# Group B's attention in a one-core decoder layer: stacked float32r scores, and two heads' value products in turns

## The chip, the cores and the metric

The kernel runs on one core of a Trainium2 chip. The metric is the time of one execution on the device, in microseconds; where several runs of a kernel are shown, their median. The engines are TensorE (PE, with its weight loads PEld), VectorE (DVE), ScalarE (ACT), GpSimd (POOL) and SyncE (SP), whose queue issues the transfers here.

## The reference, cut to what matters

One decoder layer on 512 tokens of width 1024, in float32. After an RMS norm one projection gives the inputs of two groups of 8 heads of width 64. Group A attends to the 128 keys per query that an indexer picks (top-k). Group B uses three dilated causal windows whose outputs are merged by their softmax denominators. Both outputs go through one output projection. Cross-attention into 256 memory tokens, a squared-ReLU MLP of width 4096 and a last norm follow.

```python
h = rmsnorm(x, norm_mix_g[l])
proj = h @ w_in[l]
o_a = dsa_sparse_attention(q_nope, q_rope, c_kv, k_rope, q_idx, k_idx, p_wi, w_uk[l], w_uv[l])
q_b = rope(qkv[:, :, 0]).transpose(0, 2, 1, 3)
k_b = rope(qkv[:, :, 1]).transpose(0, 2, 1, 3)
o_b = dilated_attention(q_b, k_b, v_b).transpose(0, 2, 1, 3)
x = x + heads @ w_out[l]
```

## The kernel before, in words

Tokens are taken in 4 tiles (t) or query blocks (b) of 128. Dense products are made of float32r parts: each operand is split into hi and lo, and `mm3` (L155) adds hi x hi, hi x lo and lo x hi, 8 chunks of the contraction each, into one PSUM bank of 512 columns. Weights come in units through three raw buffers on SP's queue (`load_weight`, L132); ScalarE or VectorE rounds hi, GpSimd or VectorE subtracts for lo (`split_unit`, L123). All matmuls are issued from one helper, L107, all transposes from L112, so the profile's rows are told apart by tiles: mm is a dense product, sc a score, tp a transpose, pv a value product.

PSUM has 3 banks for mm, 2 for tp, 2 for sc and 1 for pv.

Before the attention, lines 285 to 361 make the latents, the indexer's key and queries and its scores per block (`acc`). The indexer's queries are already stored as hi in partitions 0 to 63 and lo in 64 to 127 (L334 to L338). Then group B's values are projected (L364), and its queries and keys (L370 to L385): 8 heads at a time, a token tile each; `rope` (L256) rotates on VectorE into `tok`, four transposes follow, and ScalarE copies them (L383) into float32 tiles qB (buffer u2a) and kB (u2b), a pair of heads in the two halves of the partitions.

`attend` (L390) does one query block of one group, n = 128 (b + 1) keys. Head by head (two at a time in short blocks) it computes the scores, adds the bias and takes the row maximum on VectorE (L407), exponentials with their sums on ScalarE (L409), the reciprocal (L410) and the scaling (L412) on VectorE, transposes the probabilities in blocks of 128, and copies them from PSUM (pT): on ScalarE (L422) for group B, on VectorE (L420) for two thirds of group A's. The value products follow, one head's key blocks in a row, an even head in columns 0 to 63 of the array and an odd one in 64 to 127:

```python
for h, c in hs:
    r0 = (h % 2) * DH
    for kc in range(b + 1):
        mmul(pvv[r0:r0 + DH, h // 2, :], vtile[kc // 2][:, kc % 2, h * DH:(h + 1) * DH],
             pT[:, c.start + kc * P:c.start + (kc + 1) * P], start=kc == 0, stop=kc == b)
```

Group B's scores are float32 products on 64 rows of the array (`scores_b`, L436). Group A's have 96 rows (`scores_a`, L530).

Other parts: `queries_a` (L443) projects group A's queries, four heads at a time. `norm_mem` (L460) loads and normalises the memory tokens, the first of its two tiles in buffer ghi1. `keys_a` (L484) makes group A's keys and values from the latents. `top_k` (L521) runs 16 times a search for the 8 largest values and a replacement, on VectorE (L525, L526). `keys_cross` (L536) projects the memory's keys into u2a and u2b. The written order is group_b(0), queries_a(0), top_k(1), group_b(1), top_k(2), queries_a(1), memory, group_b(2), keys_a, top_k(3), group_b(3), then group A's blocks 0 to 3, keys_cross, and the output projection (`project_add`, L579), which needs both groups' heads of a token tile. This is not the order on the engines: the program is built with `schedule_with_timeline_sim=True`, and a planner that puts its own durations on instructions orders each engine's queue up to line 665; from there on products and transposes of some stages are kept in the written order (`ordered`). A queue works in order.

Of the kernel before, what the change touches and what calls it, by code (L numbers as in the profile page):

```python
# [11 lines left out]
F32 = mybir.dt.float32  # L12
# [5 lines left out]
P = 128  # L18
# [26 lines left out]
def shape_constants():  # L45
    """Tables that depend on positions alone: group B's log-multiplicity bias, the causal
    bias of a diagonal block, and the rotary cosines and sines."""
# [17 lines left out]
def kernel(  # L65
# [40 lines left out]
    def mmul(*a, **k):  # L106
        ins = nc.tensor.matmul(*a, **k)  # L107
        if ordered[0]:
            tc.keep_in_program_order(ins)

# [12 lines left out]
    def split_unit(raw, hi, lo, how="v"):  # L123
        """float32r hi and lo of raw; how names the engines: p the lo on GpSimd, v on VectorE,
        their capitals the hi on VectorE instead of ScalarE."""
        if how in "PV":
            nc.vector.tensor_copy(hi, raw)  # L127
        else:
            nc.scalar.copy(hi, raw)  # L129
        (nc.gpsimd if how in "pP" else nc.vector).tensor_tensor(lo, raw, f32(hi), op=ALU.subtract)  # L130

    def load_weight(w, segs, k0, how, between=None):  # L132
        """w [rows, cols] in DRAM; the column segments side by side, K chunks k0..k0+7.
        Returns (hi, lo): lists over the K chunks of [128, ncols] views."""
# [20 lines left out]
    def mm3(dst, a, b, first=True, last=True, ks=None):  # L155
        """dst += sum_k a_k^T b_k, a and b as (hi list, lo list); lo x lo is below float32."""
# [6 lines left out]
    # ---- RMS norms: the gain is applied where the rows are transposed; a row's 1/rms is kept  # L163
    # apart and applied where the row's products come back ----
# [19 lines left out]
    def mean_square(src, junk, n=D, scale=None):  # L184
        """Mean of a row's squares over n columns, as this part of it adds to it."""
        ms = small("ss")
        nc.scalar.activation(junk, src, AF.Square, scale=n ** -0.5 if scale is None else scale, accum_out=ms)
        return ms
# [13 lines left out]
    def transpose_half(rows, g0, his, los, bank=bank_tp):  # L202
        """rows [128 tokens, 4 chunks of 128] -> transposed, times the gain, as hi + lo per chunk."""
# [11 lines left out]
    # =============================== token mixing ===============================  # L215
# [4 lines left out]
    xa = [mtile([P, 2, D], F32, f"u2{c}") for c in "ab"]  # L220
    nc.sync.dma_start(xa[0][:, 0, 0:512], x_rows[:, 0, 0:512])
    load_gains([norm_mix_g], G_MIX)
    nc.sync.dma_start(xa[0][:, 0, 512:], x_rows[:, 0, 512:])
    w_in0 = w_in[0]

    def x_load(t):
        nc.sync.dma_start(xa[t // 2][:, t % 2, :], x_rows[:, t, :])
# [12 lines left out]
    for t in range(NT):  # L240
        xt = xa[t // 2][:, t % 2, :]
# [13 lines left out]

    def rope(ps, heads, half, tabs, t, dst, dup=None):  # L256
        """ps [128, heads, 2, half] (token rows, before the norm's 1/rms) -> dst like it, rotated
        by the token's position."""
# [3 lines left out]
        rb = tmp.tile([P, 512], F32, name=nm("rb"), tag="rb", bufs=2)  # L262
# [107 lines left out]
    qkB = []  # L370
    for tag, col in (("u2a", C_QB), ("u2b", C_KB)):
        dst = mtile([P, 4, S], F32, tag)
        wt = load_weight(w_in0, [(col, col + 512)], 0, "pppp")
        for t in range(NT):
# [8 lines left out]
            nc.scalar.copy(dst[:, :, t * P:(t + 1) * P], tp)  # L383
        qkB.append(dst)
    qB, kB = qkB  # L385
# [4 lines left out]
    def attend(b, scores, bias_of, scale, vtile, chunk0, pv):  # L390
        """One block of 128 queries, all heads of a group; leaves the heads' outputs transposed
        (features on partitions) in chunks chunk0.. of the output projection's input."""
        n = P * (b + 1)
        pvv = pv.rearrange("p (j t) -> p j t", j=4)
        per = 2 if b == 0 or b == 1 and chunk0 else 1
        order = list(range(NH)) if chunk0 == 0 else [
            q + r + 2 * i for q in range(0, NH, 2 * per) for r in range(2) for i in range(per)]
        for g in range(NH // per):
            hs = [(h, slice(n * i, n * i + n)) for i, h in enumerate(order[per * g:per * g + per])]
            ps = bank_s()  # L400
            for h, c in hs:
                scores(ps[:, c], b, h, n)
            pr = (att.tile([P, 512], F32, name=nm("p"), tag="ct0", bufs=1) if chunk0 == 0 and g % 4 == 3 else
                  att.tile([P, 512], F32, name=nm("p"), tag="p", bufs=3))
            mx, sm, rc = (small(k, 4)[:, :per] for k in ("mx", "sm", "rc"))
            for i, (h, c) in enumerate(hs):
                nc.vector.tensor_tensor_reduce(pr[:, c], ps[:, c], bias_of(b, n), op0=ALU.add, op1=ALU.min,  # L407
                                               scale=-scale, scalar=3.0e38, accum_out=mx[:, i:i + 1])
                nc.scalar.activation(pr[:, c], pr[:, c], AF.Exp, bias=mx[:, i:i + 1], scale=-1.0, accum_out=sm[:, i:i + 1])  # L409
            nc.vector.reciprocal(rc, sm)  # L410
            for i, (h, c) in enumerate(hs):
                nc.vector.tensor_scalar(pr[:, c], pr[:, c], rc[:, i:i + 1], None, op0=ALU.mult)  # L412
            tp = bank_tp()
            m = n * per
            for c in range(0, m, P):
                tpose(tp[:, c:c + P], pr[:, c:c + P], ident)
            pT = (att.tile([P, 512], F32, name=nm("pT"), tag="ct1", bufs=1) if chunk0 == 0 and g % 3 == 2 else
                  att.tile([P, 512], F32, name=nm("pT"), tag="pT", bufs=2))
            if chunk0 == 0 and g % 3 != 1:
                nc.vector.tensor_copy(pT[:, :m], tp[:, :m])  # L420
            else:
                nc.scalar.copy(pT[:, :m], tp[:, :m])  # L422
            for h, c in hs:
                r0 = (h % 2) * DH
                for kc in range(b + 1):
                    mmul(pvv[r0:r0 + DH, h // 2, :], vtile[kc // 2][:, kc % 2, h * DH:(h + 1) * DH],
                         pT[:, c.start + kc * P:c.start + (kc + 1) * P], start=kc == 0, stop=kc == b)
        for i in range(2):
            q = chunk0 // 2 + i
# [6 lines left out]
    def scores_b(dst, b, h, n):  # L436
        r0 = (h % 2) * DH
        mmul(dst, qB[r0:r0 + DH, h // 2, b * P:(b + 1) * P], kB[r0:r0 + DH, h // 2, :n],
                         start=True, stop=True)

# [33 lines left out]
    def group_b(b):  # L474
        attend(b, scores_b, lambda b, n: m3[:, 512 - n:], SC_B, vB, 4, bank("pv", 1))
# [8 lines left out]
    def keys_a():  # L484
        """Group A's keys and values from the latents."""
# [35 lines left out]
    def top_k(b):  # L521
# [5 lines left out]
        sel[b] = att.tile([P, n], F32, name=f"sel{b}")  # L527
# [315 lines left out]
```

## Time and profile before

| what | value |
|---|---|
| median of 3 runs | 846.05 us (845.87 to 847.75) |
| span of the profiled execution, first to last instruction | 843.6 us |
| the profiled execution's own time | not given apart from the span |
| PE busy | 821.7 us, 97% |
| DVE busy | 474.4 us, 56% |
| ACT busy | 331.4 us, 39% |
| POOL busy | 293.2 us, 35% |

A busy PE is not a PE at its peak: matmuls are pipelined and their ends are modelled, so the distance between the starts of records tells what one costs. The chain of waits follows the work that ended last back in time; where an engine's share stands on it, that engine's own work set the pace. A float32 product appears as two records, a float32r product as one.

### The profile page before, as it was taken

What the parts mean: (1) busy time and instruction counts of PE and PEld (TensorE: products, weight loads), DVE (VectorE), ACT (ScalarE), POOL (GpSimd) and SP (SyncE); (2) the same over time, 40 slices, a digit from 0 to 9 for tenths busy, and PEclk for the clock granted to TensorE, in tenths of its full rate; (3) what the DMA queues carried; (4) which work ended last, traced back from release to release, by engine and by line L of the source; (5) the groups of instructions that cost most, each with busy time, mean ns of one, the idle gap of its engine ahead of it and who ended that gap; (6) DMA issues with size and microseconds to landing.
All of it is one profiled execution on the core that took longest, in us unless ns stands there. A gap on an engine that the chain in (4) does not pass through costs nothing.

```text
span 843.6 us, 11086 instructions
## 1 busy us (share of the span) xinstructions
PE 821.7 (97%) x4182; PEld 679.2 (81%) x4182; DVE 474.4 (56%) x1010; ACT 331.4 (39%) x676; POOL 293.2 (35%) x179
## 2 busy tenths in 40 slices
PE   7899999999999999999999999999999999999997
PEld 6788787886787788788898878888888888888886
DVE  7876999998777634535673344423542244225413
ACT  5354424457754524223464433213431243123322
POOL 5734303131513405544501233333333333333351
PEclk9899999999999999999999999999999999999999
DMA  7443122112412303332510223333233322322202
GB/s 278 125 125 88 33 74 70 63 21 80 150 53 99 96 5 100 99 100 86 184 56 19 82 100 101 101 99 100 100 100 99 100 100 97 103 91 85 99 1 100
DMA packets 44516, 77.34 MB, mean 92 GB/s; under 512 B 4752, under 2 KB 10544, under 8 KB 44464
## 3 DMA queue, kind: packets, MB, share of 16 engines
q1 hardware_dynamic: 44464, 76.64, 27.8%
q8 instruction: 33, 0.54, 0.3%
q14 instruction: 19, 0.16, 0.1%
HBM read 74.01 MB, written 2.10 MB: 90 GB/s over the span
## 4 chain that ended last, share of the span: by engine, by line
PE 85%; DVE 11%; issue 1%; POOL 1%; ACT 1%; DMA 0%; SPq 0%; POOLq 0%; ACTq 0%; DVEq 0%
PE mm L107 71%; PE tp L112 5%; PE sc L107 5%; PE pv L107 4%; DVE m L525 1%; DVE ghi L360 1%; DVE tok L279 1%; DVE glo L526 1%; DVE rb L271 1%; DVE tok L271 1%; DVE whi L127 1%; DVE wlo L130 1%; DVE ghi L526 1%; DMA u2a<-in_x_dram 0%; DVE ghi L358 0%
## 5 line engine op out<-in xcount | busy, mean ns | idle before, releaser
L130 POOL TENSOR_TENSOR wlo<-wraw,whi 128x1024 fp32r<-128x1024 f32 (+2 forms) x107 | 256.2, 2408 | 404.5 <-ACT whi L129 318.8
L107 PE MATMUL mm<-whi,h 128*128 128x512 f32 (+2 forms) x624 | 200.1, 381 | 3.9 <-DVE h L213 2.0
L129 ACT CAST whi<-wraw 128x1024 fp32r<-128x1024 f32 (+3 forms) x111 | 114.3, 1030 | 149.6 <-PE mm L107 105.4
L107 PE MATMUL mm<-h,whi 128*128 128x512 f32 (+1 forms) x448 | 154.9, 369 | 0.0
L107 PE MATMUL mm<-wlo,h 128*128 128x512 f32 (+2 forms) x376 | 141.9, 379 | 0.2 <-DVE wlo L130 0.2
L107 PEld LDWEIGHTS mm<-whi,h 128*128 128x128 f32 x624 | 117.9, 195 | 22.0 <-ACT whi L129 2.2
L107 PE MATMUL mm<-u,whi 128*128 128x512 f32 x320 | 124.7, 390 | 0.0
L107 PE MATMUL mm<-u,wlo 128*128 128x512 f32 x320 | 123.5, 389 | 0.0
L107 PE MATMUL mm<-whi,ghi 128*128 128x512 f32 (+1 forms) x264 | 102.0, 390 | 0.0
L107 PE MATMUL mm<-whi,glo 128*128 128x512 f32 (+1 forms) x264 | 101.5, 385 | 0.0
L107 PE MATMUL mm<-wlo,ghi 128*128 128x512 f32 (+1 forms) x264 | 100.7, 383 | 0.0
L107 PEld LDWEIGHTS mm<-h,whi 128*128 128x128 f32 x448 | 81.1, 188 | 14.3 <-issue 1.0
L130 DVE TENSOR_TENSOR wlo<-wraw,whi 128x1024 fp32r<-128x1024 f32 (+2 forms) x24 | 62.2, 2591 | 37.5 <-ACT whi L129 37.5
L107 PEld LDWEIGHTS mm<-wlo,h 128*128 128x128 f32 x376 | 72.6, 194 | 11.1 <-DVE wlo L130 0.6
L107 PEld LDWEIGHTS mm<-u,whi 128*128 128x128 f32 x320 | 60.1, 188 | 12.4
L107 PEld LDWEIGHTS mm<-u,wlo 128*128 128x128 f32 x320 | 60.0, 188 | 12.5
L802 DVE TENSOR_TENSOR sq<-r 128x512 f32<-128x512 f32 x32 | 22.0, 689 | 66.7 <-ACT r L800 66.7
L107 PEld LDWEIGHTS mm<-whi,glo 128*128 128x128 f32 x264 | 49.6, 188 | 10.1 <-issue 0.2
L107 PEld LDWEIGHTS mm<-wlo,ghi 128*128 128x128 f32 x264 | 49.7, 188 | 9.6 <-issue 0.4
L107 PEld LDWEIGHTS mm<-whi,ghi 128*128 128x128 f32 x264 | 49.6, 188 | 9.4 <-issue 0.2
L409 ACT ACTIVATE p<-p,mx 128x128 f32<-128x128 f32 (+3 forms) x64 | 35.8, 560 | 29.4 <-DVE mx L407 28.5
L800 ACT ACTIVATE r<-mm 128x512 f32<-128x512 f32 x32 | 19.1, 598 | 64.8 <-PE mm L107 64.8
(212 smaller groups left out, 1116.7 us busy)
## 6 DMA issues: line engine op xcount, KB each, us to landing
wraw<-in_w_up_dram SPq DMA_DIRECT2D x32, 512.0 KB, 3.8
wraw<-in_w_down_dram SPq DMA_DIRECT2D x32, 512.0 KB, 3.6
wraw<-in_w_in_dram SPq DMA_DIRECT2D x16, 512.0 KB, 3.6
wraw<-in_w_kv_cross_dram SPq DMA_DIRECT2D x16, 512.0 KB, 3.9
wraw<-in_w_out_dram SPq DMA_DIRECT2D x8, 512.0 KB, 3.6
wraw<-in_w_q_cross_dram SPq DMA_DIRECT2D x8, 512.0 KB, 3.6
wraw<-in_w_o_cross_dram SPq DMA_DIRECT2D x8, 512.0 KB, 4.1
wraw<-in_w_in_dram SPq DMA_DIRECT2D x8, 256.0 KB, 2.9
```

Source lines behind the costliest of these rows:

```text
L107: ins = nc.tensor.matmul(*a, **k)
L112: ins = nc.tensor.transpose(*a, **k)
L127: nc.vector.tensor_copy(hi, raw)
L129: nc.scalar.copy(hi, raw)
L130: (nc.gpsimd if how in "pP" else nc.vector).tensor_tensor(lo, raw, f32(hi), op=ALU.subtract)
L271: nc.vector.scalar_tensor_tensor(o, i, r, tab, op0=ALU.mult, op1=ALU.mult)
L279: nc.vector.tensor_tensor(dst[:, :, c, :], ra[:, :, c, :], rbv[:, :, c, :], op=ALU.add)
L360: nc.vector.scalar_tensor_tensor(acc[b], rl[:, :n], wh, acc[b], op0=ALU.mult, op1=ALU.add)
L409: nc.scalar.activation(pr[:, c], pr[:, c], AF.Exp, bias=mx[:, i:i + 1], scale=-1.0, accum_out=sm[:, i:i + 1])
L526: nc.vector.match_replace(acc[b], m8, acc[b], GONE)
L800: nc.scalar.activation(r, ps, AF.Relu)
L802: nc.vector.tensor_tensor(sq, r, r, op=ALU.mult)
```

## The change

Group B's queries and keys are projected by four heads at a time (`heads_b(g)`, g = 0 and 1): a weight of 256 query and 256 key columns, kept transposed in one float32r tile, hi in partitions 0 to 63 and lo in 64 to 127, ScalarE writing hi and VectorE lo. For each query block two transfers on SP's queue write the queries with the halves exchanged (`qs`). A head's scores are two float32r products on all 128 rows: queries with keys (hi x hi and lo x lo), then exchanged queries with keys (lo x hi and hi x lo).

`attend` takes pairs of heads. In blocks 0 and 1 a pair shares one score bank, one probability tile and one copy, on ScalarE and VectorE in turns; in blocks 2 and 3 each head has its own, the first's copy on VectorE and the second's on ScalarE. The value products of the two heads are issued in turns, key block by key block, and the first one of a pair waits for both copies. There are 3 probability buffers in all (before 3, and one more for group A) and 4 of pT (before 2, and one more for group A).

The order of the work is new, as the diff's end shows. To make room, u2 becomes one buffer of 16 KB a partition, used by x, group B's first four heads, the second four, and keys_cross in that order; the rotation's scratch moves into buffer ghi1; the selection mask is bfloat16; two tiles of the residual are loaded into a pool that opens behind the attention's. Comments are removed.

```diff
...
-    xa = [mtile([P, 2, D], F32, f"u2{c}") for c in "ab"]
+    xa = mtile([P, NT, D], F32, "u2")
...
+    rbs = mtile([P, 2, 512], F32, "ghi1")
+    turn = [0]
     def rope(ps, heads, half, tabs, t, dst, dup=None):
         cos, sin, nsin = (tab[:, t, None, :].to_broadcast([P, heads, half]) for tab in tabs)
         r = r_mix[:, t:t + 1]
         n = heads * 2 * half
-        rb = tmp.tile([P, 512], F32, name=nm("rb"), tag="rb", bufs=2)
+        turn[0] ^= 1
+        rb = rbs[:, turn[0], :]
...
-    qkB = []
-    for tag, col in (("u2a", C_QB), ("u2b", C_KB)):
-        dst = mtile([P, 4, S], F32, tag)
-        wt = load_weight(w_in0, [(col, col + 512)], 0, "pppp")
+    def heads_b(g):
+        qk = mtile([P, NH, S], F32R, "u2")
+        wt = load_weight(w_in0, [(C_QB + 256 * g, C_QB + 256 * g + 256), (C_KB + 256 * g, C_KB + 256 * g + 256)], 0, "pppp")
         for t in range(NT):
             ps = bank_mm()
             mm3(ps, h_tok(t), wt)
...
             for j in range(4):
                 tpose(tp[:, j, :], tok[:, j * P:(j + 1) * P], ident)
-            nc.scalar.copy(dst[:, :, t * P:(t + 1) * P], tp)
-        qkB.append(dst)
-    qB, kB = qkB
+            for i in range(2):
+                src = tp[i * DH:(i + 1) * DH]
+                dst = qk[:, i::2, t * P:(t + 1) * P]
+                nc.scalar.copy(dst[0:DH], src)
+                nc.vector.tensor_tensor(dst[DH:P], src, f32(dst[0:DH]), op=ALU.subtract)
+        return qk
     heads_hi = [None] * 4
     heads_lo = [None] * 4
-    def attend(b, scores, bias_of, scale, vtile, chunk0, pv):
+    def attend(b, pairs, scores, bias_of, scale, vtile, q0):
         n = P * (b + 1)
-        pvv = pv.rearrange("p (j t) -> p j t", j=4)
-        per = 2 if b == 0 or b == 1 and chunk0 else 1
-        order = list(range(NH)) if chunk0 == 0 else [
-            q + r + 2 * i for q in range(0, NH, 2 * per) for r in range(2) for i in range(per)]
-        for g in range(NH // per):
-            hs = [(h, slice(n * i, n * i + n)) for i, h in enumerate(order[per * g:per * g + per])]
-            ps = bank_s()
-            for h, c in hs:
-                scores(ps[:, c], b, h, n)
-            pr = (att.tile([P, 512], F32, name=nm("p"), tag="ct0", bufs=1) if chunk0 == 0 and g % 4 == 3 else
-                  att.tile([P, 512], F32, name=nm("p"), tag="p", bufs=3))
-            mx, sm, rc = (small(k, 4)[:, :per] for k in ("mx", "sm", "rc"))
-            for i, (h, c) in enumerate(hs):
-                nc.vector.tensor_tensor_reduce(pr[:, c], ps[:, c], bias_of(b, n), op0=ALU.add, op1=ALU.min,
+        pvv = bank("pv", 1)[:, :P * len(pairs)].rearrange("p (j t) -> p j t", t=P)
+        one = 2 * n <= 512
+        for at, j in enumerate(pairs):
+            if one:
+                bk, pr = bank_s(), att.tile([P, 512], F32, name=nm("p"), tag="p", bufs=3)
+                sc, prs = [bk[:, :n], bk[:, n:2 * n]], [pr[:, :n], pr[:, n:2 * n]]
+            else:
+                sc = [bank_s()[:, :n] for _ in range(2)]
+                prs = [att.tile([P, 512], F32, name=nm("p"), tag="p", bufs=3)[:, :n] for _ in range(2)]
+            for i in range(2):
+                scores(sc[i], b, 2 * j + i, n)
+            mx, sm, rc = (small(k, 4)[:, :2] for k in ("mx", "sm", "rc"))
+            for i in range(2):
+                nc.vector.tensor_tensor_reduce(prs[i], sc[i], bias_of(b, n), op0=ALU.add, op1=ALU.min,
                                                scale=-scale, scalar=3.0e38, accum_out=mx[:, i:i + 1])
-                nc.scalar.activation(pr[:, c], pr[:, c], AF.Exp, bias=mx[:, i:i + 1], scale=-1.0, accum_out=sm[:, i:i + 1])
+                nc.scalar.activation(prs[i], prs[i], AF.Exp, bias=mx[:, i:i + 1], scale=-1.0, accum_out=sm[:, i:i + 1])
             nc.vector.reciprocal(rc, sm)
-            for i, (h, c) in enumerate(hs):
-                nc.vector.tensor_scalar(pr[:, c], pr[:, c], rc[:, i:i + 1], None, op0=ALU.mult)
-            tp = bank_tp()
-            m = n * per
-            for c in range(0, m, P):
-                tpose(tp[:, c:c + P], pr[:, c:c + P], ident)
-            pT = (att.tile([P, 512], F32, name=nm("pT"), tag="ct1", bufs=1) if chunk0 == 0 and g % 3 == 2 else
-                  att.tile([P, 512], F32, name=nm("pT"), tag="pT", bufs=2))
-            if chunk0 == 0 and g % 3 != 1:
-                nc.vector.tensor_copy(pT[:, :m], tp[:, :m])
+            for i in range(2):
+                nc.vector.tensor_scalar(prs[i], prs[i], rc[:, i:i + 1], None, op0=ALU.mult)
+            if one:
+                tp, pT = bank_tp(), att.tile([P, 512], F32, name=nm("pT"), tag="pT", bufs=4)
+                for i in range(2):
+                    for c in range(0, n, P):
+                        tpose(tp[:, i * n + c:i * n + c + P], prs[i][:, c:c + P], ident)
+                if at % 2:
+                    nc.vector.tensor_copy(pT[:, :2 * n], tp[:, :2 * n])
+                else:
+                    nc.scalar.copy(pT[:, :2 * n], tp[:, :2 * n])
+                pTs = [pT[:, :n], pT[:, n:2 * n]]
+                both = None
             else:
-                nc.scalar.copy(pT[:, :m], tp[:, :m])
-            for h, c in hs:
-                r0 = (h % 2) * DH
-                for kc in range(b + 1):
-                    mmul(pvv[r0:r0 + DH, h // 2, :], vtile[kc // 2][:, kc % 2, h * DH:(h + 1) * DH],
-                         pT[:, c.start + kc * P:c.start + (kc + 1) * P], start=kc == 0, stop=kc == b)
-        for i in range(2):
-            q = chunk0 // 2 + i
+                pTs = []
+                for i in range(2):
+                    tp, pT = bank_tp(), att.tile([P, 512], F32, name=nm("pT"), tag="pT", bufs=4)
+                    for c in range(0, n, P):
+                        tpose(tp[:, c:c + P], prs[i][:, c:c + P], ident)
+                    if i:
+                        both = nc.scalar.copy(pT[:, :n], tp[:, :n])
+                    else:
+                        nc.vector.tensor_copy(pT[:, :n], tp[:, :n])
+                    pTs.append(pT)
+            for kc in range(b + 1):
+                for i in range(2):
+                    h = 2 * j + i
+                    ins = mmul(pvv[i * DH:(i + 1) * DH, at, :], vtile[kc // 2][:, kc % 2, h * DH:(h + 1) * DH],
+                               pTs[i][:, kc * P:(kc + 1) * P], start=kc == 0, stop=kc == b)
+                    if both is not None and kc == 0 and i == 0:
+                        tc.add_manual_dep(ins.ins, both.ins.name, mybir.DependencyInfo(
+                            mybir.DependencyClass.Sync, mybir.DependencyReason.DATA), reason="the pair in turns")
+        for i in range(len(pairs) // 2):
+            q = q0 + i
             if heads_hi[q] is None:
                 heads_hi[q] = mtile([P, 2, S], F32R, f"ghi{q}")
                 heads_lo[q] = mtile([P, 2, S], F32R, f"glo{q}")
             bsl = slice(b * P, (b + 1) * P)
             split_from(pvv[:, 2 * i:2 * i + 2, :], heads_hi[q][:, :, bsl], heads_lo[q][:, :, bsl])
-    def scores_b(dst, b, h, n):
-        r0 = (h % 2) * DH
-        mmul(dst, qB[r0:r0 + DH, h // 2, b * P:(b + 1) * P], kB[r0:r0 + DH, h // 2, :n],
-                         start=True, stop=True)
...
-    def group_b(b):
-        attend(b, scores_b, lambda b, n: m3[:, 512 - n:], SC_B, vB, 4, bank("pv", 1))
+    def group_b(g, qk, b):
+        bsl = slice(b * P, (b + 1) * P)
+        qs = att.tile([P, 4, P], F32R, name=nm("qs"), tag="qs", bufs=2)
+        nc.sync.dma_start(f32(qs[0:DH]), f32(qk[DH:P, 0:4, bsl]))
+        nc.sync.dma_start(f32(qs[DH:P]), f32(qk[0:DH, 0:4, bsl]))
+        def scores_b(dst, b, h, n):
+            mmul(dst, qk[:, h % 4, bsl], qk[:, 4 + h % 4, :n], start=True, stop=False)
+            mmul(dst, qs[:, h % 4, :], qk[:, 4 + h % 4, :n], start=False, stop=True)
+        attend(b, [2 * g, 2 * g + 1], scores_b, lambda b, n: m3[:, 512 - n:], SC_B, vB, 2 + g)
...
-        sel[b] = att.tile([P, n], F32, name=f"sel{b}")
+        sel[b] = att.tile([P, n], BF16, name=f"sel{b}")
...
     def group_a(b):
-        attend(b, scores_a, lambda b, n: sel[b], SC_A, state["vA"], 0, bank("pv", 1))
+        attend(b, [0, 1, 2, 3], scores_a, lambda b, n: sel[b], SC_A, state["vA"], 0)
...
     def keys_cross(i):
         memT = state["memT"]
         if i == 0:
-            state["kc"] = [mtile([P, KD, MEM], F32R, f"u2{c}") for c in "ab"]
+            kk = mtile([P, 2, KD, MEM], F32R, "u2")
+            state["kc"] = [kk[:, c] for c in range(2)]
...
-    group_b(0)
+    qk = heads_b(0)
+    group_b(0, qk, 0)
+    top_k(1)
+    group_b(0, qk, 1)
     queries_a(0)
-    top_k(1)
-    group_b(1)
+    group_b(0, qk, 2)
     top_k(2)
+    group_b(0, qk, 3)
     queries_a(1)
+    qk = heads_b(1)
     memory()
-    group_b(2)
+    group_b(1, qk, 0)
+    group_b(1, qk, 1)
     keys_a()
     top_k(3)
-    group_b(3)
+    group_b(1, qk, 2)
+    group_b(1, qk, 3)
     for b in range(NT):
         group_a(b)
     for i in range(2):
         keys_cross(i)
     memT, kc, res = state["memT"], state["kc"], state["res"]
-    xr = [mtile([P, D], F32, f"u3{'ab'[t]}") if t < 2 else res.tile([P, D], F32, name=f"xr{t}") for t in range(NT)]
+    p1b.close()
+    p2 = ctx.enter_context(tc.tile_pool(name="tmp2", bufs=1, reuse_waits="tile"))
+    xr = [mtile([P, D], F32, f"u3{'ab'[t]}") if t < 2 else p2.tile([P, D], F32, name=f"xr{t}") for t in range(NT)]
     for t in range(NT):
         nc.sync.dma_start(xr[t], x_rows[:, t, :])
-    p1b.close()
...
```

## Rows read from the trace of the kernel before

**Rows 1.** The page's opening: span, busy time, share and instructions of each engine.

```profile
span 843.6 us, 11086 instructions
...
PE 821.7 (97%) x4182; PEld 679.2 (81%) x4182; DVE 474.4 (56%) x1010; ACT 331.4 (39%) x676; POOL 293.2 (35%) x179
```

**Rows 2.** Busy time by stretch: its length, each engine, PE clock, DMA share.

```profile
80.00:235.00 155.00, 150.92 (x846) 120.08 (x844) 142.81 (x436) 76.13 (x185) 44.39 (x23) 0.99 0.24 73
235.00:310.00 75.00, 75.00 (x513) 60.16 (x513) 48.67 (x139) 36.72 (x94) 19.47 (x9) 1.00 0.22 71
310.00:843.60 533.60, 524.93 (x2469) 438.62 (x2467) 223.58 (x283) 179.71 (x310) 188.13 (x108) 1.00 0.27 91
```

**Rows 3.** Chain of waits from 80 to 310 us, shares by line.

```profile
by line: PE mm L107 32.6%; PE pv L107 15.9%; PE sc L107 13.9%; PE tp L112 12.0%; DVE m L525 4.6%; DVE ghi L360 4.2%; DVE tok L279 3.6%; DVE glo L526 2.9%; DVE tok L271 2.6%; DVE rb L271 2.4%; DVE ghi L526 2.1%; DVE ghi L358 1.4%; issue 1.0%
```

**Rows 4.** Chain of waits in order of time: start, us, what.

```profile
222.50 0.58 PE pv L107 x4
...
226.67 1.02 PE pv L107 x8
...
255.19 2.14 PE mm L107 x18
...
290.67 0.44 PE tp L112 x4
...
303.91 0.59 PE tp L112 x4
...
307.26 4.80 PE mm L107 x21
```

**Rows 5.** PE in order of time, from 293 us: start, us, line, operation, tiles.

```profile
293.98 0.27 PE L107 MATMUL pv<-pT,vAb 128*64 128x128 f32 x1
293.99 0.32 PE L107 MATMUL pv<-pT,vAa 128*64 128x128 f32 x1
294.09 0.27 PE L107 MATMUL pv<-pT,vAb 128*64 128x128 f32 x1
294.15 0.27 PE L107 MATMUL pv<-pT,vAa 128*64 128x128 f32 x1
```

**Rows 6.** PE by form, group B's scores: busy us, mean ns of one.

```profile
L107 PE MATMUL sc<-u2b,u2a 64*128 64x512 f32 x16 | 6.7, 641 | 0.0
...
L107 PE MATMUL sc<-u2b,u2a 64*128 64x384 f32 x16 | 6.1, 535 | 0.2
...
L107 PE MATMUL sc<-u2b,u2a 64*128 64x256 f32 x16 | 2.3, 402 | 0.0
...
L107 PE MATMUL sc<-u2b,u2a 64*128 64x128 f32 x16 | 1.9, 304 | 0.0
```

**Rows 7.** PE in order of time, from 16.4 us.

```profile
16.75 0.27 PE L107 MATMUL mm<-wlo,h 128*128 128x232 f32 x1
16.85 0.39 PE L107 MATMUL mm<-whi,h 128*128 128x232 f32 x2
```

**Rows 8.** VectorE lines L338, L412, L420: xcount, ns min/median/max, start, forms.

```profile
L338 DVE TENSOR_TENSOR u<-tp,u x6: 683/689/695, 49.5 to 60.9; 64x512 fp32r<-64x512 f32 x6
...
L412 DVE TENSOR_SCALAR p<-p,rc x64: 274/409/2061, 142.0 to 294.5; 128x128 f32<-128x128 f32 x16, 128x256 f32<-128x256 f32 x16, 128x384 f32<-128x384 f32 x16, 128x512 f32<-128x512 f32 x16
...
L420 DVE COPY pT<-tp x18: 410/552/692, 233.4 to 302.4; 128x256 f32<-128x256 f32 x8, 128x384 f32<-128x384 f32 x5, 128x512 f32<-128x512 f32 x5
```

**Rows 9.** VectorE by form, 0 to 312 us: busy us, mean ns of one.

```profile
L525 DVE MAX8 m<-ghi 128x8 f32<-128x512 f32 x16 | 11.0, 688 | 0.2
L526 DVE MATCH_REPLACE8 ghi<-m,ghi 128x512 f32<-128x512 f32 x16 | 10.8, 674 | 0.0
...
L410 DVE RECIPROCAL rc<-sm 128x1 f32<-128x1 f32 x40 | 6.4, 160 | 7.3 <-ACT p L409 7.2
```

**Rows 10.** DMA issues: KB each, median us from issue to landing.

```profile
wraw<-in_w_in_dram SPq DMA_DIRECT2D x8, 128.0 KB, 2.8
...
ghi<-in_mem_dram SPq DMA_DIRECT2D x1, 512.0 KB, 6.3
```

More of the change, by code (lines that the diff above doesn't have):

```diff
@@ L109, in mmul @@
             tc.keep_in_program_order(ins)
+        return ins
     def tpose(*a, **k):
@@ L218 @@
     tmp = p1a.enter_context(tc.tile_pool(name="tmp1", bufs=1))
-    xa = [mtile([P, 2, D], F32, f"u2{c}") for c in "ab"]
-    nc.sync.dma_start(xa[0][:, 0, 0:512], x_rows[:, 0, 0:512])
+    xa = mtile([P, NT, D], F32, "u2")
+    nc.sync.dma_start(xa[:, 0, 0:512], x_rows[:, 0, 0:512])
     load_gains([norm_mix_g], G_MIX)
-    nc.sync.dma_start(xa[0][:, 0, 512:], x_rows[:, 0, 512:])
+    nc.sync.dma_start(xa[:, 0, 512:], x_rows[:, 0, 512:])
     w_in0 = w_in[0]
     def x_load(t):
-        nc.sync.dma_start(xa[t // 2][:, t % 2, :], x_rows[:, t, :])
+        nc.sync.dma_start(xa[:, t, :], x_rows[:, t, :])
     wa = load_weight(w_in0, [(C_CKV, C_KR + DR), (C_KI, C_WI + NH)], 0, "vpvp", between=lambda u: x_load(1 + u))
@@ L240 @@
     for t in range(NT):
-        xt = xa[t // 2][:, t % 2, :]
+        xt = xa[:, t, :]
         tsl = slice(t * P, (t + 1) * P)
@@ L565 @@
     memT, kc, res = state["memT"], state["kc"], state["res"]
-    xr = [mtile([P, D], F32, f"u3{'ab'[t]}") if t < 2 else res.tile([P, D], F32, name=f"xr{t}") for t in range(NT)]
+    p1b.close()
+    p2 = ctx.enter_context(tc.tile_pool(name="tmp2", bufs=1, reuse_waits="tile"))
+    xr = [mtile([P, D], F32, f"u3{'ab'[t]}") if t < 2 else p2.tile([P, D], F32, name=f"xr{t}") for t in range(NT)]
     for t in range(NT):
         nc.sync.dma_start(xr[t], x_rows[:, t, :])
-    p1b.close()
-    p2 = ctx.enter_context(tc.tile_pool(name="tmp2", bufs=1, reuse_waits="tile"))
     r_cross = p2.tile([P, NT], F32, name="r_cross")
@@ L784 @@
             hh = mtile([P, KD, S], F32R, "h0")
-            hl = [mtile([P, 4, S], F32R, f"u2{c}") for c in "ab"]
+            hl = mtile([P, KD, S], F32R, "u2")
             hid_hi = [hh[:, k, :] for k in range(KD)]
-            hid_lo = [hl[k // 4][:, k % 4, :] for k in range(KD)]
+            hid_lo = [hl[:, k, :] for k in range(KD)]
         else:
```

## The prediction, made before the run

> **What bounds the kernel now.** I read the page first, then the busy times by stretch, then the chain of waits. TensorE (PE) is busy 97% of an 843.6 us span [rows 1]. The stretches show that the change touches three of them and leaves the last one, 533.6 us of dense products from 310 us on, alone [rows 2]. From 80 us to 310 us, PE is busy 226 of 230 us at a granted clock of 0.99 to 1.00, that is at its 2.4 GHz level. But VectorE (DVE) is no easy second: from 80 to 235 us, where the two groups' projections, the top-k search and group B's attention lie, it is busy 142.8 of 155 us; only behind 235 us, in group A's attention, does it fall to 48.7 of 75 [rows 2]. The chain from 80 to 310 us goes 15.9% through value products (pv) and 13.9% through scores (sc) on PE [rows 3], and 24% through DVE steps of the search, the indexer and the rotation. So PE time removed counts as long as DVE can still feed it.
>
> The execution profiled has no time of its own beside its span of 843.6 us; the median of the three runs is 846.05, 2.45 us above it for what lies around. I take that difference as fixed and give results on the scale of the median.
>
> **The change part by part.**
>
> *Value products in turns.* A float32 product is two records on PE: 8 heads x 10 key blocks x 2 groups are 320 pv records. 15.9% of 230 us is 36.6 us of chain for them [rows 3]. A run of 4 takes 0.58 us, one of 8 takes 1.02 [rows 4]: 0.11 a record and 0.14 fixed. What follows pays as well: four transposes take 0.59 us behind another kind of tile and 0.44 otherwise [rows 4], so 0.15. The chain has 44 pv pieces between 80 and 310 us, of the kind of rows 4, which makes 36.6 + 44 x 0.15 = 43.2 us now. Where the order happens to put two heads side by side, the trace already shows what the change wants: records alternate between the halves at 293.98, 293.99, 294.09 and 294.15 us, two every 0.11 us [rows 5]. After: 160 pairs of records x 0.11 = 17.4 us, and 32 runs (4 pairs x 4 blocks x 2 groups) x 0.29 = 9.3, together 26.7. Saving: 16.5 us, of which 11 before 235 us and 5 behind it, by where the pieces lie. Ends: 0, if halves don't overlap, and 20, if runs of neighbouring pairs merge.
>
> *Group B's scores.* Now 64 records on half the rows, 6.7 + 6.1 + 2.3 + 1.9 = 17.0 us busy [rows 6], of which I count 16 on the path (the rest is tails under the next instruction), and some 16 pieces with 0.15 us behind each: 18.4. After, 64 float32r products on the whole array, with no change of tile: 512 columns take 4.80 / 21 = 0.229 us, 256 take 2.14 / 18 = 0.119 [rows 4], 384 lie between at 0.174. For 128 columns there is no such row; 232 columns are 0.10 us apart [rows 7] and a transpose of 128 takes 0.11 [rows 4], so it lies between 0.05 (by columns) and 0.21 (twice a transpose); I take 0.11, the nearer row. 16 x (0.229 + 0.174 + 0.119 + 0.11) = 10.1 us. Saving 8 us, all before 235 us (7 to 9 by the unknown).
>
> PE in all: **24.5 us less**, 19 before 235 us and 5 behind. The projections keep their products.
>
> *VectorE.* The lo parts are 16 new instructions on 64 partitions x 512, for which the indexer's query split has the same form: 0.689 us [rows 8], 11.0 us. Copies of transposed probabilities: for group B none were on DVE; after, half are: 2 x 0.41 + 2 x 0.69 + 4 x 0.55 + 4 x 0.69 = 7.2 us by the durations of rows 8. For group A 18 copies (9.5 us) become 12 (7.2). Reciprocals fall from 52 to 32, at 0.16 us [rows 9]: -1.3 for B, -1.9 for A. Before 235 us that is 11.0 + 7.2 - 1.3 = **16.9 us more**, behind it 4 us less. The steps that scale probabilities on DVE take 0.27 to 2.06 us with a median of 0.41 [rows 8], while the 6 splits of the new kind lie within 0.683 and 0.695. The Trainium skill, page "SBUF — State Buffer", section "Who interferes with whom", says that a VectorE instruction with at most one SBUF input, outside its two-port modes, does not contend with GpSimd. By it the added splits, which read one operand from PSUM, stay at 0.69 us; were they stretched as the scaling steps are, some microseconds would be added. The trace agrees so far, with only 6 of them.
>
> *ScalarE.* Eight more copies for the hi parts, and the pT copies it loses, about cancel; it is busy 76 of 155 us [rows 2]: nothing, covered.
>
> *DMAs.* Sixteen transfers of 128 KB swap the halves of the queries; a weight segment of that size takes 2.8 us [rows 10]. They wait on the lo split, and on SP's queue weight loads stand behind them. Bounds: 0, if the scores come later than the transfer by other work in PE's order, and 8 blocks x 2.8 = 22 us, if each second score product waits in PE's in-order queue with everything behind it. Only a group's first block is needed soon after its split; I take 1 us. The memory tokens' first tile now loads behind the last rotation, since its buffer holds the rotation's scratch: 6.3 us [rows 10] at about 190 us, needed by keys_cross some 45 us later: 0, and at most those 6.3. The late residual loads, of 512 KB like that one, are needed at the third output tile, 11 us into that projection: 0, same bound.
>
> *What PE then waits for.* Before 235 us PE's work falls from 151 to 132 us while DVE's rises from 143 to 160, more than the 155 us there are. If all of DVE's work has to be done before group B ends, PE idles 28 us, less some 8.6 us of keys_cross that can run ahead into three PSUM banks (24 products x 0.119 each, [rows 4]; its results wait for the buffer that group B's scores still read): 20. If the last block's search (11.0 + 10.8 us, [rows 9]), wanted only by group A's last block, slips behind 235 us, where DVE has room, the idle time is about 6. The written order puts it ahead of group B's last two blocks, but other work goes between its steps. I take the middle: **14 us given back**, the 1 us of DMA in it. Late next, in that stretch, is DVE.
>
> Sum: 846 - 24.5 + 14 = 835.5, **836**.
>
> **The rivals.**
>
> *PE keeps the pace throughout.* Then nearly all 24.5 us stay: 822 to 828. For it: PE's gaps are 4 us of 155 now [rows 2], and the search, which nothing waits for early, fills DVE. Against: 160 us of work in 155. Chance 0.2.
>
> *DVE takes over and the time gets longer.* Attention on DVE waits for ScalarE's exponentials; with three probability buffers used in pairs it can hide less. If it works at 90% of its time from 80 us on, 160 us take 177 and group B ends 22 us later; group A gives back 5, keys_cross ahead 8.6: 846 + 8 = 854. At 94%, 170 us, it is 15 - 13.6: 847. Below about 94% it is slower than before; now it stands at 92% there with PE in the lead. The Trainium skill's page "TensorEngine Tiling (Array Packing)", section "PSUM Bottleneck", says that tiling speeds up TensorE but not PSUM evacuation; by that rule this case is the one, at 847 to 854. The trace bears it out in part: the copies and splits that read PSUM grow while PE's part shrinks, but 48.7 of 75 us behind 235 us shows room. Chance 0.27: slower 0.17, equal 0.10.
>
> *The halves don't overlap in turns*, since both records of a product come before the other head's. Then pv is 320 x 0.11 + 9.3 = 44.5, only the scores gain, DVE's wait shrinks to about 5: 843. Against it: rows 5, where two streams run side by side. Chance 0.03.
>
> **How the numbers follow.** The forecast, most of PE's gain with part given back (829 to 843), has 0.50; rivals 0.20, 0.27 and 0.03. A measurement of this kernel can tell about 0.3% from no change, 2.5 us. Faster: 0.50 + 0.20 + half of the last rival, less 0.03 of the forecast's own upper edge, 0.69; same: 0.10 + 0.03 and the other half of the last, 0.14; slower 0.17. The range of 8 in 10 goes from 823, which leaves out the end of the first rival, to 850, which leaves out the longer half of the second.
>
> **What would show it.** Right: pv records two every 0.11 us in 32 runs or fewer; no 64-row scores; score products of 512 columns at 0.23 us; DVE at 95% or more from 80 us to group B's end; PE gaps of some 14 us there that end on DVE's rows; everything behind the attention unchanged, moved by 10 us. Wrong: pv records still 0.11 us apart; gaps that end on the query swap; or no gaps at all, which would be the first rival.

## The result, and the profile after

The changed kernel takes **865.9 us** (median of 4 runs, 862.8 to 867.1), the kernel before 846.6 in runs beside it: a ratio of 1.0226, 95% interval 1.0204 to 1.0249. It is 2.3% slower, where 836 was forecast. The opening of the changed kernel's page:

```profile
span 865.3 us, 11158 instructions
...
PE 816.7 (94%) x4182; PEld 680.3 (79%) x4182; DVE 493.0 (57%) x1012; ACT 329.0 (38%) x674; POOL 293.4 (34%) x179
```

Against [rows 1] PE's share has fallen from 97% to 94%, and DVE has 19 us more to do. Group B's last value product lies at 261.0 us (before 234.8), group A's at 328.4 (before 306.6). Busy times by stretch, cut at those ends (columns as in [rows 2]):

```profile
80.00:205.00 125.00, 111.37 (x610) 95.33 (x609) 121.02 (x331) 44.23 (x96) 24.31 (x12) 0.95 0.22 62
205.00:261.00 56.00, 42.60 (x268) 33.49 (x266) 45.80 (x126) 32.47 (x92) 21.83 (x12) 0.79 0.38 104
261.00:330.00 69.00, 66.02 (x489) 51.90 (x484) 45.25 (x121) 35.53 (x92) 19.55 (x9) 1.00 0.29 92
330.00:865.30 535.30, 526.63 (x2476) 440.21 (x2474) 224.71 (x286) 180.29 (x312) 188.21 (x109) 1.00 0.29 91
```

Behind group A's last value product the time is as it was: 536.9 us to the end, before 537.0. All of the loss lies ahead of 261 us: group B ends 26.2 us later, and group A then takes 67.4 us instead of 71.8. From 80 us to group B's end DVE is busy 121.0 + 45.8 = 166.8 of 181 us, which is 92%; before it was 142.8 of 155, 92% too. PE idles 27 of those 181 us, before 4 of 155 [rows 2]. In the second stretch its granted clock is 0.79 on average, and cut finer (the same view):

```profile
200.00:206.60 6.60, 6.51 (x34) 5.30 (x33) 6.27 (x14) 2.33 (x4) 0.00 (x0) 1.00 0.00 1
206.60:212.40 5.80, 0.63 (x4) 0.40 (x4) 4.48 (x9) 1.16 (x2) 0.00 (x0) 0.73 0.82 167
212.40:226.00 13.60, 10.76 (x43) 7.91 (x44) 9.10 (x38) 9.59 (x32) 7.37 (x6) 0.50 0.32 85
```

PE does four transposes in 5.8 us, and then runs at 0.50, the 1.2 GHz level, for 13.6 us. What it waited for, 80 to 262 us (us in total, times, longest), and the chain of waits over the same stretch (shares by line, then two of its pieces: start, us, what):

```profile
PE tp L113 <- DVE p L422: 8.6, 6, 2.0
PE sc L107 <- DMA qs<-u: 5.2, 1, 5.2
PE sc L107 <- DVE mx L417: 3.1, 4, 1.9
```

```profile
by line: PE mm L107 16.0%; DVE m L556 9.9%; DVE p L422 8.2%; DVE ghi L557 6.8%; PE tp L113 6.3%; DVE ghi L365 5.1%; PE pv L107 4.4%; DVE u L393 4.2%; DVE glo L557 4.0%; PE sc L107 3.9%; DVE tok L276 3.5%; DVE p L417 3.2%; DVE ghi L276 3.0%;
...
207.11 5.22 DMA qs<-u
...
254.83 1.02 PE pv L107 x16
```

In [rows 3] the products and transposes of PE had 74.4% and the search 9.6 (L525, L526); now the search (L556, L557) has 20.7%, and the scaling of probabilities (L422) 8.2. The last line shows the turns: 16 records of value products take 1.02 us, where 8 did before [rows 4]. Two scores in PE's order of time, the two products of one head in block 3; then DVE by form from 80 to 262 us, where L393 are the lo splits:

```profile
229.87 0.50 PE L107 MATMUL sc<-u 128*128 128x512 f32 x1
230.21 0.40 PE L107 MATMUL sc<-u,qs 128*128 128x512 f32 x1
```

```profile
L393 DVE TENSOR_TENSOR u<-tp,u 64x512 fp32r<-64x512 f32 x16 | 11.0, 689 | 4.7 <-ACT u L392 4.3
...
L422 DVE TENSOR_SCALAR p<-p,rc 128x384 f32<-128x384 f32 x8 | 8.4, 1078 | 0.0
```

### The profile page after: what moved, and what is told of

Read it like the earlier page. It is cut to its first block, busy times and chain, and to the rows that moved or that the text cites. A ratio compares the mean times of both kernels' runs of the same rounds, so it can differ in the third digit from the quotient of the medians.

```text
span 865.3 us, 11158 instructions
## 1 busy us (share of the span) xinstructions
PE 816.7 (94%) x4182; PEld 680.3 (79%) x4182; DVE 493.0 (57%) x1012; ACT 329.0 (38%) x674; POOL 293.4 (34%) x179
## 4 chain that ended last, share of the span: by engine, by line
PE 73%; DVE 18%; issue 2%; ACT 2%; DMA 2%; POOL 1%; POOLq 0%; ACTq 0%; DVEq 0%
PE mm L107 64%; PE tp L113 4%; PE sc L107 3%; DVE p L422 2%; DVE m L556 2%; PE pv L107 2%; DVE ghi L557 1%; POOL wlo L131 1%; DVE ghi L365 1%; DVE whi L128 1%; DVE u L393 1%; DMA wraw<-in_w_o_cross_dram 1%; DVE glo L557 1%; DVE p L417 1%; DVE wlo L131 1%
## 5 line engine op out<-in xcount | busy, mean ns | idle before, releaser
L107 PE MATMUL mm<-h,whi 128*128 128x512 f32 (+1 forms) x448 | 153.0, 366 | 0.0
L107 PEld LDWEIGHTS mm<-whi,h 128*128 128x128 f32 x624 | 120.1, 199 | 21.6 <-ACT whi L130 2.2
L107 PEld LDWEIGHTS mm<-wlo,h 128*128 128x128 f32 x376 | 73.8, 197 | 10.8 <-DVE wlo L131 0.5
L107 PE MATMUL mm<-whi,u 128*128 128x512 f32 x128 | 49.8, 389 | 0.0
L419 ACT ACTIVATE p<-p,mx 128x128 f32<-128x128 f32 (+3 forms) x64 | 35.7, 559 | 27.4 <-DVE mx L417 24.9
```

The costliest lines, as they stand in the source:

```text
L419: nc.scalar.activation(prs[i], prs[i], AF.Exp, bias=mx[:, i:i + 1], scale=-1.0, accum_out=sm[:, i:i + 1])
```

## The experiments

In the texts of the first four runs theory A is VectorE with the search ahead of the attention, B the sum of VectorE's work, C the swap of the halves and the probability buffers. From the run without the search on, A is VectorE being full up to 205 us, B the swap, C the memory tokens' load, which now comes behind the last rotation. Ratios are to the kernel before, with 95% intervals.

**Each half of the change alone.** The stacked scores with their order, on the old `attend` (the diff is the change without the `attend` part):

> The changed kernel with the attention of before (one head's value products in a row, its copies and buffers), so the stacked scores, the exchange and the new order alone. Theory A: the new order with its searches costs most: 858 to 870. Theory B: VectorE has 11 us more and PE 8 us less work: 848 to 856. Theory C, as far as it blames the pairs: 846 to 850.

Measured: 864.5, ratio 1.0202 [1.0185, 1.0219], in theory A's range and, within the spread of the runs, as slow as the whole change. Group B ends at 252.4 us (before 234.8). So most of the loss comes with the stacked scores and what they bring along; the turns, added to them, move group B's end on to 261.0 us and give 6 us back in group A. Now the turns alone, on the kernel before (its scores and order, the new `attend`):

> The kernel before with the value products in turns alone (pairs of heads, the new copies and buffers), group B's scores, projections and order as before. Theories A and B: PE saves 16 us of value products, VectorE gains only copies, about 5 us net: 832 to 842. Theory C, as far as it blames three probability buffers in pairs: 847 or more.

Measured: 854.0, ratio 1.0085 [1.007, 1.01]. The value products' starts add up to 23.9 us instead of 36.6, and yet the kernel is 8 us slower, in theory C's range: group B ends at 247.0 us (before 234.8), while group A then takes 67.2 us instead of 71.8. So the turns pay in group A and lose in group B.

**Where the search is written.** The three `top_k` calls moved to right before the `group_a` block that needs each:

```diff
-    top_k(3)
...
     for b in range(NT):
+        if b:
+            top_k(b)
         group_a(b)
```

> The changed kernel with only the written place of the top-k searches moved: each stands right ahead of the block of group A that needs it. Same instructions. Theory A (VectorE paces the stretch, and the searches stand ahead of the steps that PE waits for): 20 us or so come back, 840 to 852. Theory B (the sum of VectorE's work decides, in whatever order): within 5 us of 866. Theory C (PE waits for the query exchange and for buffers, not for VectorE's turn): within 5 us of 866.

Measured: 865.7, ratio 1.022 [1.0199, 1.0242]. It tested nothing of the theory: the planner issued the search from 80 to 202 us as in the changed kernel, since it was ready. The written place is no handle on it.

**Less work on VectorE.** The scaling of probabilities on ScalarE, in both groups:

```diff
-                nc.vector.tensor_scalar(prs[i], prs[i], rc[:, i:i + 1], None, op0=ALU.mult)
+                nc.scalar.activation(prs[i], prs[i], AF.Copy, scale=rc[:, i:i + 1])
```

> The changed kernel with the scaling of the probabilities on ScalarE instead of VectorE: some 42 us of VectorE time (with its collisions with GpSimd) become some 34 us of ScalarE time. Theories A and B: VectorE no longer paces, 830 to 845. Theory C (exchange, three probability buffers in pairs): the chain of one pair gets no shorter, 858 or more.

Measured: 862.5, ratio 1.0186 [1.017, 1.0201]. VectorE lost 39 us of work from 80 to 330 us (23 of them before group B's end, which came 5.8 us sooner) and the kernel only 3: VectorE's amount of work is not all that holds the changed kernel up. Then the search itself left out (the two instructions in `top_k`'s loop):

> The changed kernel without the 48 steps of search and replacement per query row (the threshold step stays, the mask is then wrong); all else as it is. That takes some 54 us from VectorE between 80 and 205 us. Theory A: PE's own work sets the pace up to 205 us, group B ends some 25 us sooner, and the time falls to 830 to 845. Theory B: the waits from 206 us on remain, 852 to 860. Theory C: the same, 852 to 860.

Measured: 849.7, ratio 1.0045 [1.003, 1.006]: 16 us less, 5 us short of theory A's range. A stall and half clock at 192 us remain.

**The swap** left out (`qs[:, h % 4, :]` becomes `qk[:, h % 4, bsl]`, no transfers):

> The changed kernel without the transfers that swap the halves of the queries; the second score product takes the queries as they are (the cross terms hi x lo and lo x hi are left out, the number of products stays). Theory A (VectorE is full up to about 205 us, with 120 of 125 us busy, and hands everything over late): the swap is on the chain for 5.2 us once, so 859 to 864. Theory B (the swap is the cause: its transfers wait on SyncE's queue with the weight loads behind them, the first score products of the second four heads wait 5.2 us, and PE then runs at half clock for 17 us): 844 to 853, and no half-clock stretch behind 205 us. Theory C (the memory tokens' load behind the last rotation holds up ScalarE's queue): 860 to 865.

Measured: 864.0, ratio 1.0213 [1.0191, 1.0235]: 2 us, less than the runs of the changed kernel differ among themselves (862.8 to 867.1). Theory B falls as the main cause. The 17 us of half clock at 209 us stay, and the chain there now goes through the next thing that was late, "DMA ghi<-in_mem" and ScalarE's squares of the memory tokens (L188).

**The memory tokens** in buffers that are free early:

```diff
-            mraw = mtile([P, D], F32, ("ghi1", "glo1")[t])
+            mraw = mtile([P, D], F32, ("glo0", "glo1")[t])
```

> The changed kernel with the memory tokens' two tiles in two buffers that are free early, so that the load doesn't wait for the rotation's scratch. Theory A and theory B: 864 to 867, no change. Theory C: the squares of the memory tokens leave ScalarE's queue between 206 and 218 us, the copies and exponentials behind them start sooner, 855 to 861.

Measured: 860.9, ratio 1.0178 [1.016, 1.0195], 5 us less; the clock from 205 to 260 us is 0.91 on average instead of 0.78. This is ScalarE's queue in the changed kernel, in order of time (L188 squares the memory tokens, L419 is the exponential; between the squares and it comes a copy of a hi part):

```profile
215.38 1.05 ACT L188 ACTIVATE junk<-ghi 128x1024 bf16<-128x1024 f32 x1
...
216.43 1.04 ACT L188 ACTIVATE junk<-glo 128x1024 bf16<-128x1024 f32 x1
...
218.07 0.40 ACT L419 ACTIVATE p<-p,mx 128x128 f32<-128x128 f32 x1
```

The first exponential of the second four heads stands behind two squares; with the early load they are gone from this place and it starts at 215.37.

**All three** (no search, no swap, early memory tokens):

> The changed kernel without the search, without the swap of the halves (both left out as in the two runs above) and with the memory tokens' tiles in early buffers. If the three together are all that holds PE up, PE's own time remains: 822 to 832. If each only takes what it gave alone, 865.9 - 16 - 5 - 2 = 843. If what remains is the place of group B's second four heads (their attention from about 206 us on has few dense products beside it, and PE falls to half clock there): 840 to 848, with a stall and half clock in that stretch still.

Measured: 838.8, ratio 0.992 [0.9905, 0.9935]: 27 us less, a little more than the 23 of the sum. A stall and 10 us of half clock at 192 us are left, at the last rotations and first scores of the second four heads. The next run put group A's last queries beside them (`queries_a(1)` and `memory()` written behind `group_b(1, qk, 0)`):

> The changed kernel with the memory tokens in early buffers and the written order changed so that the second half's projection comes before group A's last queries, whose dense products then lie beside the attention of the second four heads. If the lack of dense products beside that attention costs time: 846 to 855, with PE's clock at 1.00 from 205 to 260 us. If VectorE's amount of work sets the end of group B wherever it is put: 858 to 862, as with early memory tokens alone (860.9).

Measured: 857.2, ratio 1.0133 [1.0117, 1.015]: 4 us less than with early memory tokens alone, neither forecast. The clock there is 0.91, not 1.00, and it was 0.91 with the early tokens alone: that the dense products gave the 4 us by way of the clock is not shown.

**What the kernel before can bear.** The search left out of the kernel before:

> The kernel before without the 48 steps of search and replacement (the threshold step stays, the mask is then wrong). If the search holds up the kernel before no less than the changed one: 828 to 834, as much as the 16 us there. If VectorE is behind PE only by the change: 840 to 846.

Measured: 845.3, ratio 0.9984 [0.9974, 0.9993]: 1.4 us. And the kernel before with the change's 16 lo splits besides:

```diff
             nc.scalar.copy(dst[:, :, t * P:(t + 1) * P], tp)
+            for i in range(2):
+                nc.vector.tensor_tensor(spare[i * DH:(i + 1) * DH], tp[i * DH:(i + 1) * DH],
+                                        dst[i * DH:(i + 1) * DH, :, t * P:(t + 1) * P], op=ALU.subtract)
```

> The kernel before with the 16 lo splits of the change besides, 11.0 us of VectorE written to a spare tile that nothing reads (and the bfloat16 mask, to make room). If VectorE's amount of work sets the end of group B, at 92% of its time as before: 11 / 0.92 = 12 us later there, 5 to 12 us in the end, 851 to 858. If PE sets it and VectorE has slack: 846 to 849.

Measured: **857.8**, ratio 1.0136 [1.0119, 1.0153]. 11.0 us of work that nothing reads cost 11.2. The splits could also have cost time by keeping the transposes' PSUM banks longer; but by the profile nothing waited for a split, and PE's longest wait from 80 to 250 us is for VectorE's rotation (us in total, times, longest):

```profile
PE tp L112 <- DVE tok L279: 4.9, 2, 4.7
```

Busy times from 80 to 205 us, first the kernel before, then without the search, then with the splits:

```profile
80.00:205.00 125.00, 120.92 (x660) 98.39 (x659) 119.83 (x373) 56.19 (x138) 29.60 (x17) 0.99 0.21 61
```

```profile
80.00:205.00 125.00, 124.41 (x668) 99.49 (x667) 75.06 (x233) 57.03 (x141) 30.20 (x17) 1.00 0.22 61
```

```profile
80.00:205.00 125.00, 118.76 (x625) 96.75 (x623) 120.75 (x361) 53.44 (x129) 30.42 (x18) 0.97 0.22 63
```

Without the search VectorE falls to 75 us, and PE does hardly more by 205 us (668 records for 660): PE sets the pace. With the splits VectorE stays near its 120, and PE is 35 records behind. The kernel before stands where both engines are full: without the whole search on VectorE it gains 1.4 us, and 11 us more there cost their full time.

**Mending.** Scaling on ScalarE with early memory tokens:

> The changed kernel with the scaling on ScalarE and the memory tokens in early buffers. If ScalarE's queue, held by the squares of the memory tokens, ate what VectorE's relief gave: 843 to 853. If the relief is worth 3 us wherever it stands: 857 to 859.

Measured: 849.4, ratio 1.0032 [1.002, 1.0044]. The same relief of VectorE that gave 3 us now gives 11.6 (from 860.9). With the scaling alone on ScalarE, its queue had stood 3.1 us for the memory tokens and then done their squares at 209 us, and the first exponential of the second four heads followed at 212.0; here that starts at 202.5. With the dense products beside and a fourth probability buffer for group A too:

> The changed kernel with memory tokens early, dense products beside the second four heads, scaling on ScalarE, and the fourth probability buffer for group A. If the single gains add: 865.9 - 5 - 4 - 3 - 3 = 851. If the relief of VectorE pays once the queues are free: 835 to 845. If stacked scores can't pay in this place: not below 850.

Measured: 846.4, ratio 0.9996 [0.9987, 1.0005]. Mended in four places the change comes out even.

**The turns where they pay.** On the kernel before, pairs and turns in group A alone:

> The kernel before with the pairs and turns in group A alone; group B and the order as before. If the turns save where VectorE has room (group A took 67.2 us from group B's last value product to its own in the run with turns in both groups, 71.8 before), 846 - 4.6 = 841 to 843. If pairs in three probability buffers cost more than the turns save in any stretch: 846 to 850.

Measured: 842.7, ratio 0.9962 [0.9949, 0.9975]. With the fourth probability buffer:

```diff
+                prs = [(att.tile([P, 512], F32, name=nm("p"), tag="ct0", bufs=1) if at % 2 and i else
+                        att.tile([P, 512], F32, name=nm("p"), tag="p", bufs=3))[:, :n] for i in range(2)]
```

> The run with turns in group A alone (842.7), with the fourth probability buffer that the kernel before has for group A. If three buffers held group A's pairs up: 839 to 841.5. If PE's own time sets the pace there: 842 to 843.5.

Measured: **839.9**, ratio 0.9931 [0.9916, 0.9946], faster than both kernels. Group B ends at 234.6 us as before, group A 64.9 us later instead of 71.8. Three buffers did hold the pairs up. In the two rows below (235 to 310 us, three and four buffers) PE goes from 72.4 to 75.0 of 75 us:

```profile
235.00:310.00 75.00, 72.36 (x528) 58.38 (x526) 46.45 (x123) 38.27 (x97) 19.82 (x10) 1.00 0.25 85
```

```profile
235.00:310.00 75.00, 75.00 (x541) 61.14 (x541) 46.40 (x128) 39.01 (x101) 19.79 (x10) 1.00 0.25 85
```

**Turns in group B.** Turns in both groups, group B's copies on ScalarE as in the kernel before:

> The run with turns in both groups on the kernel before (854.0), with group B's copies of transposed probabilities all on ScalarE as in the kernel before. If VectorE's 7 us of copies are what made it slower: 842 to 847. If pairs with three probability buffers and two score banks are: 851 to 855.

Measured: 850.4, ratio 1.0056 [1.0041, 1.0071], 3.6 us less than with half of the copies on VectorE: half of the step. The scaling of group B on ScalarE as well, with turns in both groups (and the fourth buffer for group A), and with turns in group A alone:

> Turns in both groups on the kernel before, group B's copies and its scaling on ScalarE, the fourth probability buffer for group A. If VectorE's amount is what made turns in group B slower: 16 to 20 us less on it, and 830 to 838. If pairs lose in group B by their buffers: 843 to 849.

> Turns in group A alone with the fourth probability buffer (839.9), and group B's scaling on ScalarE. PE was at its limit when the search was left out of the kernel before (845.3 against 846.7), so relief of VectorE alone gives little: 838 to 840. If VectorE holds PE up there: 830 to 836.

Measured: 847.6, ratio 1.0037 [1.0008, 1.0067], and 846.9, ratio 1.0009 [0.9999, 1.0018]. Both forecasts for relief fail: on ScalarE the scaling makes the kernel 6.9 us slower than 839.9, though VectorE then has 110.8 us to do by 205 us instead of 119.8. Turns in group B change nothing beside it. Why the scaling costs that on ScalarE there, and why pairs don't pay in group B, was not settled; group B's scores and transposes start further apart (by the sums of their distances, 20.9 and 20.8 us instead of 17.7 and 18.3), in no single wait.

## Why the prediction was wrong

*Value products: right.* 26.7 us were forecast, some 22 of them without what follows each run (160 x 0.11 is 17.6, not 17.4). The distances between starts of all 320 records add up to 27.7 us after (before 36.6), with 3.6 us of waits and 4.6 us in stretches at clock 0.50 among them; the run with turns on the kernel before shows 23.9. The halves overlap.

*Group B's scores: near in size, lost in place.* Where one score of 512 columns follows another at clock 1.00, their starts are 0.23 us apart, as forecast, in three of seven cases, and 0.34 in the other four, as in the rows above. By the means of each form at that clock and without waits, the 64 would take some 12 us (an estimate) instead of 10.1. They add up to 20.2, more than the 17.7 before, since 4.3 us of waits for what follows them (the scaling and copies of probabilities) and 7.9 us in stretches at clock 0.50 fell among them.

*VectorE: 16.9 us more were forecast, 24 came* (166.8 against 142.8 to group B's end). The splits took the 11.0 us to the digit. What was missed is the scaling: 64 steps took 42.0 us instead of 33.0 over both groups, and all of the 9 us fell before group B's end; in group B 128x384 took 1.08 us on average instead of 0.42. The steps are long where GpSimd subtracts a weight's lo part:

```profile
235.62 5.08 DVE L422 TENSOR_SCALAR p<-p,rc 128x384 f32<-128x384 f32 x2
```

```profile
230.65 9.84 POOL L131 TENSOR_TENSOR wlo<-wraw,whi 128x1024 fp32r<-128x1024 f32 x4 [6.21 <-DVE whi L128]
```

A 384-column step alone took 0.41 us; the 8 of 16 beside GpSimd took 1.70 on average and up to 2.60. The splits stayed within 683 and 695 ns, and the two of them that ran beside GpSimd took 694. The Trainium skill's page "SBUF — State Buffer", section "Who interferes with whom", separates them in this way: a tensor_scalar in a two-port mode can be blocked by GpSimd for the whole of its instruction, an instruction with one SBUF input outside those modes is not. The trace agrees on both, on the second with two cases only.

*The 14 us given back: this step failed.* 44 were given back: the 24.5 that PE was to save, and 20 beyond. It failed in three ways. First, "If all of DVE's work has to be done before group B ends, PE idles 28 us" lets VectorE work without a gap, 160 us in 160 (and 4 of the 28 were PE's idle time already, 155 less 150.9). But VectorE was idle for 12.2 of 155 us before and for 14.2 of 181 after: group B's end moved by the 24.0 us of VectorE's added work and 2 more, and the splits put into the kernel before cost 1:1 as well. The middle that was taken was not there, since the search, which was to slip behind 235 us, was done at 203; and the step's upper end, 20 us, gives only 841.5. VectorE's amount is not the only cause in the changed kernel: 23 us less of it moved group B's end by 5.8. Second, the memory tokens' load was put at "0, and at most those 6.3": with their load early the kernel takes 5 us less, and with it the same relief of VectorE gave 11.6 instead of 3. I had asked when the products need the tokens, not what stands behind their squares in ScalarE's in-order queue. Third, no term stood for PE's clock: up to the end of group A, PE's idle time grew by 26 us (4.1 of 230 before, 30.0 of 250 after), and running at half clock behind such waits cost some 12 more (an estimate: each record's distance to the next against the mean of its form at full clock). How the time splits between the three was not settled.

*DMAs, 1 us:* 2 without the swap, within the spread of the runs. Of its 5.2 us on the chain most were covered by the memory tokens: without it the first exponential of the second four heads starts at 216.4 us instead of 218.1, behind the same squares. Group B ends 5.0 us sooner in that run's profile; what gave the rest stays open.

*The rivals.* The first falls with PE's 27 us of idle time, the third with 16 records in 1.02 us. The second, VectorE takes over, is what happened; its rule of 90 to 94% held at 92% (the sign of being right, 95% or more, did not come), but it gave 847 to 854, with 160 us of work, and took off 13.6 for group A and keys_cross. Of the 26 us by which group B ends later, group A gives back 4.4 in all, and what lies behind 0.1. The Trainium skill's page "TensorEngine Tiling (Array Packing)", section "PSUM Bottleneck", spoke for it, and the splits, which read PSUM, bear it out in part: of VectorE's 120 us up to 205 us, 45 fall away without the search, which reads none. I gave this rival 0.27, because I read 92% as VectorE having 8% left. The run without the search shows PE as the bound, the run with the splits shows VectorE without reserve; one profile can't tell the two.

## What to carry to other kernels

Where two engines are both above 90% in a stretch, as here before group B's end, take the second as full until a run shows otherwise: work moved onto it cost its own time here, whatever the first one saved. Put such a change where the second engine has room (here group A, 48.7 of 75 us [rows 2], where the turns with a fourth buffer give 0.7%), and try the added work alone in the old kernel first. When a buffer is shared anew, follow the load that now waits to its first reader, and look at what is queued behind that reader.

## What had not been expected of the hardware

After 5.8 us with 0.63 us of PE's work, four transposes, PE ran at clock 0.50 through 13.6 us in which it was busy 10.8. So the waits that the change brought slowed the attention behind them as well. And moving 39 us of scaling from VectorE to ScalarE was worth 3 us in one place, 11.6 in another, and cost 6.9 in a third (group B's part of it).
